# The low part of the in-projection weight by ScalarE and an adding transfer instead of VectorE

## The chip, the cores and the metric

The kernel runs on one core of a Trainium2 chip. The metric is the device time of one execution in microseconds (us). TensorE multiplies, VectorE and ScalarE do elementwise work, GpSimd and SyncE mainly issue transfers here. In the profile these are PE (PEld for its weight loads), DVE, ACT, POOL and SP; SPq and POOLq are the queues on which SP and POOL issue transfers.

## The reference

One layer of a diffusion backbone over 1024 latent tokens of width 1024, with 256 context tokens. All arithmetic is float32. Cut to what matters here:

```python
h = modulate(rmsnorm(x, norm1_g[i]), sh1, sc1)
q, k, v, hv, hx1, hx2, gna, ghy = jnp.split(h @ w_in[i], IN_SPLITS, axis=-1)
y_na = neighbourhood_attention(to_heads(q), to_heads(k), to_heads(v), ...)
y_hy = hyena_mixer(hv, hx1, hx2, *hy_params)
x = x + g1 * gated_merge(gna, ghy, y_na, y_hy, w_na_o[i], w_hy_o[i], w_out[i])
x = x + g2 * swiglu(modulate(rmsnorm(x, norm2_g[i]), sh2, sc2), ffn_w1[i], ffn_w3[i], ffn_w2[i])
return rmsnorm(x, final_g)
```

The change is inside `h @ w_in[i]`: a 1024 x 1024 activation times a 1024 x 5120 weight (the columns of k and v also multiply the 256 context tokens).

## The kernel before, in words

**A product in three parts.** A float32 product is made from operands that are split in two. The high part is the value rounded to the format that TensorE multiplies in (float32r); the low part is the value minus its high part. `gemm` (L187 to L198) then adds three products for each block of 128 rows: low weight by high activation, high weight by low activation, high by high, all three into one PSUM bank. `split` (L173 to L176) makes the parts: ScalarE casts the value into the high part (L175), VectorE subtracts the high part from the value (L176).

**A weight chunk.** The 5120 columns of `w_in` are 40 chunks of 128 columns. `weights` (L178 to L185) brings one in: SP issues a 512 KB load into the tile `wr` (L181), then `split` fills `wh` and `wl` (128 partitions x 1024 elements each). There is one buffer for `wr` and two each for `wh` and `wl`. So a chunk's parts can be written only when the chunk two before has been multiplied to its end, and its load can start only when the previous split has read `wr`.

**The order of chunks.** `project` (L574 and on) goes through the chunks in the order 4, 5, 6 to 23, 0 to 3, 32 to 39, 24 to 31. For each it asks for the weight of the next one, under a raised priority (L643 to L645), and then runs two halves of 512 tokens, 24 matmuls each, into the tile `in_ps`. ScalarE (L591 to L614), and for the short convolution also VectorE (L600), take a half out of its bank into the tile `proj`. For eight chunks a context product `ctx_ps` follows. Finished rows are stored by POOL (`qk` L624, `gate` L631, `hx`, `z`, `vtok` L572). The first two chunks, 4 and 5, are asked for in `hidden` (L305, L313), not in `project`.

**What runs beside it.** Between the chunks a merger of generators, with costs written out by hand, mixes in other work. First come the filters of the long convolution (`filt_ps` L363, which VectorE multiplies by a decay that SP loads into `dec`, L359; then `dft_ps` L442 to L444 from the tile `a`, which VectorE makes at L430) and the modulation rows (VectorE sums 64 loads `wal`, L887 to L890). Then come the convolutions. From about 640 us attention joins: POOL loads the tile `v` (L706, 64 loads of 64 KB in all), and a little later the matmuls of projection and attention are pinned to the order of the program and `in_ps` has one bank only. The rest of the order on each engine's queue is made by the framework when the kernel is built, by priorities and modelled durations; each queue then runs strictly in that order.

**After it.** The Hyena output projection, the merge, and the feed-forward stage use weights of their own; two of these also call `weights` with 512 columns.

Of the kernel before, what the change touches and what calls it, by code (L numbers as in the profile page):

```python
# [10 lines left out]
F32 = mybir.dt.float32  # L11
F32R = mybir.dt.float32r
AF = mybir.ActivationFunctionType
ALU = mybir.AluOpType
# [5 lines left out]
D = 1024  # L20
# [138 lines left out]
class Block:  # L159
# [15 lines left out]
        self.nc.scalar.copy(hi, src)  # L175
        self.nc.vector.tensor_sub(lo, src, hi.bitcast(F32))  # L176

    def weights(self, pool, src, n=D, tag="w"):  # L178
        nc = self.nc
        raw = pool.tile([P, D], F32, tag=tag + "r", name=tag + "r")[:, :n]  # L180
        nc.sync.dma_start(raw, src)  # L181
        hi = pool.tile([P, D], F32R, tag=tag + "h", name=tag + "h")[:, :n]
        lo = pool.tile([P, D], F32R, tag=tag + "l", name=tag + "l")[:, :n]
        self.split(hi, lo, raw)
        return hi, lo  # L185

    def gemm(self, ps, w, x, nk, width=512, pos=0, pin=False):  # L187
# [386 lines left out]
    def project(self, groups, wpool, psg, psc, hT, hcT, between, then):  # L574

        nc = self.nc
        count = [0]  # L580
        chunks = [f for g in groups for f in g]
        turn = []

        def half(f, w, st, ps, h):
            sl = slice(h * 512, (h + 1) * 512)
            count[0] += 1
            pt = psg[0 if self.pinned else count[0] % 2].tile([P, 512], F32, tag="g", name="in_ps")
            ps.append(pt)
            self.gemm(pt, w, hT[h], 8, 512, 0, self.pinned)
            if f < 4:  # L590
                nc.scalar.mul(st[:, sl].rearrange("p (c r i) -> p c r i", c=4, r=8),  # L591
                              pt.rearrange("p (r c i) -> p c r i", r=8, c=4), 0.125)
            elif f < 12:
                nc.scalar.copy(st[:, sl], pt)
            elif f < 24:
                c0, c1, c2, cb = (self.cw[:, f - 12, n:n + 1] for n in range(4))
                nc.scalar.activation(st[:, sl], pt, AF.Identity, bias=cb, scale=c1)

                def tap(d0, d1, src, c):
                    nc.vector.scalar_tensor_tensor(st[:, d0:d1], src, c, st[:, d0:d1], op0=ALU.mult, op1=ALU.add)  # L600

                with self.tc.high_priority():
                    if h == 0:
                        edge = self.stg.tile([P, 1], F32, tag="edge", name="edge")
                        nc.vector.tensor_copy(edge, ps[0][:, 511:512])
                        ps.append(edge)
                        tap(1, 512, ps[0][:, 0:511], c0)
                        tap(0, 511, ps[0][:, 1:512], c2)
                    else:
                        tap(512, 513, ps[1], c0)  # L610
                        tap(513, T, ps[2][:, 0:511], c0)
                        tap(511, T - 1, ps[2], c2)
            else:
                nc.scalar.activation(st[:, sl], pt, AF.Copy if f < 32 else AF.Sigmoid)  # L614

        def finish(f, w, st):
            if 4 <= f < 12:
                pc = psc.tile([P, 512], F32, tag="c", name="ctx_ps")
                self.gemm(pc[:, 0:TC], w, hcT, 8, TC)
            for t in turn:  # L620
                self.tokens(psc, *t)
            turn.clear()
            if f < 8:
                nc.gpsimd.dma_start(self.qkd[f], st)  # L624
            elif f < 12:
                turn.append((st, 8, self.vd.rearrange("(n p) c -> p n c", p=P)[:, :, (f - 8) * P:(f - 7) * P]))
            elif f < 24:
                g, cc = (f - 12) // 4, f % 4
                turn.append((st, 8, (self.zd[0] if g == 0 else self.hxd[g - 1])[cc // 2][:, :, (cc % 2) * P:(cc % 2 + 1) * P]))
            else:  # L630
                nc.gpsimd.dma_start(self.gd[f - 24], st)  # L631
            if 4 <= f < 12:
                sc = self.stc.tile([P, TC], F32, tag="oc", name="projc")
                nc.scalar.copy(sc, pc[:, 0:TC])
                if f < 8:
                    nc.gpsimd.dma_start(self.kcd[f - 4], sc)
                else:
                    turn.append((sc, 2, self.vcd.rearrange("(n p) c -> p n c", p=P)[:, :, (f - 8) * P:(f - 7) * P]))

        for group in groups:  # L640
            i = chunks.index(group[-1]) + 1
            for f in (*group, *chunks[i:i + 1]):
                if f not in self.ready:  # L643
                    with self.tc.high_priority():
                        self.ready[f] = self.weights(wpool, self.a["w_in"][f])  # L645
            ws = [self.ready.pop(f) for f in group]
            sts = [self.stg.tile([P, T], F32, tag="o", name="proj") for _ in group]
            pss = [[] for _ in group]
            for h in range(2):
                for f, w, st, ps in zip(group, ws, sts, pss):  # L650
                    half(f, w, st, ps, h)
                    if self.fine:
                        if h:
                            self.left -= 1
                            finish(f, w, st)
                        yield
                if group is groups[0]:
                    next(between)
                if group is groups[-1] and not h:
                    then()  # L660
            if not self.fine:
                for f, w, st in zip(group, ws, sts):
                    self.left -= 1
                    finish(f, w, st)
                    yield
# [806 lines left out]
```

## Time and profile before

| what | value |
|---|---|
| device time, median of 3 runs | 1711.23 us (1708.59 to 1711.89) |
| span of the profiled execution | 1711.4 us |
| splits of `w_in` chunks | 40, the first cast at 32.5 us |
| share of the span busy: PE, DVE, ACT, POOL | 97%, 72%, 39%, 9% |
| bytes moved by transfers | 282.48 MB, mean 165 GB/s |

The span is the profiled execution's own time; it lies 0.2 us beside the median of the runs. A row of the timeline has the start in us, the length in us, the engine, the line, what is written from what, and in brackets how long the engine had been idle and what ended that. A row of a table by stretches has, for each stretch, its length, the busy time of each engine, the granted clock of TensorE (PEclk, 1.00 is full), the busy share of the 16 DMA engines and GB/s. A row of the waits reads "who waited <- for what: us in total, how many times, the longest". A row of transfers ends with KB each and the median time from issue to landing.

### The profile page before, as it was taken

Reading aid. Unit: us, or ns where it says so; the run is one execution under the profiler, and the core shown is the slowest. Engines: PE = TensorE matmul, PEld = TensorE weight load, DVE = VectorE, ACT = ScalarE, POOL = GpSimd, SP = SyncE. Lnnn points to the kernel's source line nnn. Section 1 sums busy time; section 2 is a strip of 40 time slices with the busy share of each in tenths; the row PEclk is TensorE's granted clock in tenths of the full one; section 3 lists DMA queues with packets and bytes.
Section 4 is the critical chain, followed back from the end, with each engine's and each line's share of the span. In section 5 each row is a group of like instructions: output and inputs, shape, how many; then the busy total and the mean of one; then the engine's idle time right before and its main releaser. Section 6 shows DMA issues by size and latency. Waiting matters only on the chain.

```text
span 1711.4 us, 22611 instructions
## 1 busy us (share of the span) xinstructions
PE 1657.6 (97%) x8124; PEld 1307.2 (76%) x8124; DVE 1230.1 (72%) x2076; ACT 662.6 (39%) x1141; POOL 153.3 (9%) x274
## 2 busy tenths in 40 slices
PE   6898999999999999999999999999999999999997
PEld 2676776777777778888787888888888888878886
DVE  3697586699995966465865967867865566479576
ACT  4621221312221224455654315733333333355455
POOL 0100211101010014020200000010101011000000
PEclk9999999999999999999999999999999999999999
DMA  9276854645553456344657524333423223395334
GB/s 364 103 255 199 266 173 158 215 139 187 167 201 137 160 187 186 126 148 131 197 174 245 187 65 160 124 124 117 160 99 110 94 99 109 105 383 177 98 120 154
DMA packets 114517, 282.48 MB, mean 165 GB/s; under 512 B 15840, under 2 KB 24676, under 8 KB 112102
## 3 DMA queue, kind: packets, MB, share of 16 engines
q1 hardware_dynamic: 94472, 219.99, 38.6%
q0 software_dynamic: 19280, 60.60, 10.5%
q8 instruction: 64, 1.05, 0.3%
q10 hardware_dynamic: 653, 0.44, 0.1%
q14 instruction: 48, 0.39, 0.1%
HBM read 213.60 MB, written 67.39 MB: 164 GB/s over the span
## 4 chain that ended last, share of the span: by engine, by line
PE 65%; issue 10%; DVE 4%; DMA 2%; ACT 1%; POOL 1%; SPq 0%; DVEq 0%; POOLq 0%; ACTq 0%
PE x_ps L1171 15%; PE in_ps L195 12%; PE z_ps L1171 7%; PE dx_ps L1340 6%; PE out_ps L1109 4%; PE dz_ps L1340 3%; PE hy_ps L195 2%; PE y_ps L1171 2%; PE dft_ps L442 2%; PE pt_ps L800 2%; PE pt_ps L786 2%; PE na_ps L195 2%; PE dy_ps L1340 1%; PE s_ps L766 1%; PE dft_ps L444 1%
## 5 line engine op out<-in xcount | busy, mean ns | idle before, releaser
L195 PE MATMUL in_ps<-hTh,wl 128*128 128x512 f32 x640 | 260.0, 407 | 0.9 <-ACT proj L614 0.5
L195 PE MATMUL in_ps<-hTl,wh 128*128 128x512 f32 x640 | 254.5, 398 | 0.4 <-DVE hTl L176 0.2
L195 PE MATMUL in_ps<-hTh,wh 128*128 128x512 f32 x640 | 253.9, 397 | 0.0
L195 PEld LDWEIGHTS in_ps<-hTh,wl 128*128 128x128 f32 x640 | 121.5, 190 | 32.2 <-issue 5.6
L195 PEld LDWEIGHTS in_ps<-hTl,wh 128*128 128x128 f32 x640 | 121.8, 190 | 27.1 <-DVE hTl L176 1.8
L195 PEld LDWEIGHTS in_ps<-hTh,wh 128*128 128x128 f32 x640 | 121.6, 190 | 26.9 <-issue 0.4
L175 ACT CAST wh<-wr 128x1024 fp32r<-128x1024 f32 (+1 forms) x56 | 51.9, 926 | 141.4 <-PE in_ps L195 110.0
L176 DVE TENSOR_TENSOR wl<-wr,wh 128x1024 fp32r<-128x1024 f32 (+1 forms) x56 | 59.8, 1067 | 63.2 <-ACT wh L175 63.1
L176 DVE TENSOR_TENSOR ol<-ws,oh 128x512 fp32r<-128x512 f32 x88 | 60.4, 688 | 50.6 <-ACT oh L175 50.3
L176 DVE TENSOR_TENSOR ol<-ar,oh 128x512 fp32r<-128x512 f32 x77 | 52.8, 687 | 47.7 <-ACT oh L175 47.7
L175 ACT CAST oh<-ar 128x512 fp32r<-128x512 f32 x77 | 47.9, 622 | 84.4 <-PE dx_ps L1340 33.1
L175 ACT CAST oh<-ws 128x512 fp32r<-128x512 f32 x88 | 54.7, 622 | 57.1 <-PE x_ps L1171 27.5
L442 PE MATMUL dft_ps<-a,matf 128*128 128x512 f32 x128 | 67.1, 606 | 5.0 <-DVE a L430 4.1
L775 ACT ACTIVATE pe<-pe,mx 128x640 f32<-128x640 f32 x64 | 52.6, 822 | 48.9 <-DVE mx L774 48.9
L1340 PE MATMUL dx_ps<-ol,oh 128*128 128x512 f32 x176 | 68.7, 390 | 1.7 <-DVE ol L176 1.7
L774 DVE CUSTOM_DVE_ANT_0 pe<-s_ps,bias 128x640 f32<-128x640 f32 x64 | 50.1, 820 | 28.1 <-PE s_ps L769 28.1
L1340 PE MATMUL dx_ps<-oh,ol 128*128 128x512 f32 x176 | 67.4, 390 | 1.9 <-DVE ol L176 1.9
L1340 PE MATMUL dx_ps<-oh 128*128 128x512 f32 x176 | 68.5, 389 | 0.0
L176 DVE TENSOR_TENSOR ol<-wr,oh 128x512 fp32r<-128x512 f32 x70 | 48.0, 688 | 22.3 <-ACT oh L175 22.2
L175 ACT CAST oh<-wr 128x512 fp32r<-128x512 f32 x70 | 43.3, 622 | 52.3 <-PE x_ps L1171 16.0
L890 DVE SCALAR_TENSOR_TENSOR aacc<-wal,cs,aacc 128x512 f32<-128x512 f32 x56 | 41.8, 747 | 23.1 <-DMA wal<-in_w_ada 22.5
L1111 DVE TENSOR_TENSOR x<-x,out_ps 128x512 f32<-128x512 f32 x64 | 42.6, 683 | 15.2 <-PE out_ps L1109 15.0
(394 smaller groups left out, 4193.7 us busy)
## 6 DMA issues: line engine op xcount, KB each, us to landing
wr<-in_w SPq DMA_DIRECT2D x52, 512.0 KB, 3.4
wr<-in_w_in SPq DMA_DIRECT2D x40, 512.0 KB, 4.2
ar<-g SPq DMA_DIRECT2D x77, 256.0 KB, 2.8
wal<-in_w_ada SPq DMA_DIRECT2D x64, 256.0 KB, 4.1
matf<-in_dft_f SPq DMA_DIRECT2D x32, 384.0 KB, 4.7
bias<-in_rpb SPq DMA_DIRECT2D x64, 192.0 KB, 3.7
g<-t POOLq DMA_DIRECT2D x47, 256.0 KB, 3.0
w<-in_w SPq DMA_DIRECT2D x44, 256.0 KB, 5.4
```

The costliest lines, as they stand in the source:

```text
L175: self.nc.scalar.copy(hi, src)
L176: self.nc.vector.tensor_sub(lo, src, hi.bitcast(F32))
L195: mm = nc.tensor.matmul(ps, ww[:, k * P:(k + 1) * P], xx[:, k, pos:pos + width], start=(i == 0), stop=(i == n - 1))
L442: nc.tensor.matmul(ps, m[:, 0], v.rearrange("p a b -> p (a b)"), start=True, stop=False)
L774: nc.vector.tensor_tensor_reduce(pe, ps[:, 256:896], bt, -1.0, 3e38, ALU.add, ALU.min, mx[:, 0:1])
L775: nc.scalar.activation(pe, pe, AF.Exp, bias=mx[:, 0:1], scale=-1.0, accum_out=mx[:, 1:2])
L786: pin(nc.tensor.transpose(pt[:, at:at + P], pe[:, c * P:(c + 1) * P], self.ident))
L890: nc.vector.scalar_tensor_tensor(acc, w, c, acc, op0=ALU.mult, op1=ALU.add)
L1109: nc.tensor.matmul(ps, gg[x][:, tk], ww[y][:, sl], start=(i == 0), stop=(i == n - 1))
L1111: nc.vector.tensor_add(x1[:, sl], x1[:, sl], ps)
L1171: mm = nc.tensor.matmul(ps, w[u][:, k * P:(k + 1) * P], x[v][:, k, :], start=(start and k == 0 and i == 0), stop=(stop and k == 3 and i == 2),
L1340: nc.tensor.matmul(ps[j], x[u][:, j * P:(j + 1) * P], w[v], start=(start and i == 0 and c == 0), stop=(stop and i == N - 1 and k == len(re ...
```

## The change

`weights` gets a flag, and `project` sets it. With the flag, ScalarE casts the chunk into the high part as before, then writes minus the high part into the low part's tile, and POOL issues a transfer that reads the same 512 KB of the weight from memory a second time and adds it to what stands in that tile. VectorE's subtraction is gone for these chunks. Chunks 4 and 5 and all other weights keep `split`, so 38 of the 40 chunks change.

```diff
-    def weights(self, pool, src, n=D, tag="w"):
+    def weights(self, pool, src, n=D, tag="w", by_dma=False):
         nc = self.nc
         raw = pool.tile([P, D], F32, tag=tag + "r", name=tag + "r")[:, :n]
         nc.sync.dma_start(raw, src)
         hi = pool.tile([P, D], F32R, tag=tag + "h", name=tag + "h")[:, :n]
         lo = pool.tile([P, D], F32R, tag=tag + "l", name=tag + "l")[:, :n]
-        self.split(hi, lo, raw)
+        if by_dma:
+            nc.scalar.copy(hi, raw)
+            nc.scalar.mul(lo, hi.bitcast(F32), -1.0)
+            nc.gpsimd.dma_start(lo, src, accum_op=ALU.add)
+        else:
+            self.split(hi, lo, raw)
         return hi, lo
...
                 if f not in self.ready:
                     with self.tc.high_priority():
-                        self.ready[f] = self.weights(wpool, self.a["w_in"][f])
+                        self.ready[f] = self.weights(wpool, self.a["w_in"][f], by_dma=True)
```

## The prediction

> **What bounds the kernel now.** I read the page's head first, then the busy time by stretches, then what TensorE (PE) waits for.
>
> ```profile
> span 1711.4 us, 22611 instructions
> ...
> PE 1657.6 (97%) x8124; PEld 1307.2 (76%) x8124; DVE 1230.1 (72%) x2076; ACT 662.6 (39%) x1141; POOL 153.3 (9%) x274
> ```
>
> PE is busy for 97% of the span, VectorE (DVE) for 72%. An average over stages says nothing about this change, so here is the stage in which the changed chunks are multiplied (columns: stretch and its length, busy PE, PEld, DVE, ACT, POOL, granted clock, share of the DMA engines, GB/s).
>
> ```profile
> 30.00:100.00 70.00, 62.73 (x328) 47.40 (x325) 48.46 (x80) 39.00 (x66) 6.79 (x14) 0.98 0.50 177
> 100.00:200.00 100.00, 92.74 (x432) 68.58 (x431) 78.31 (x113) 20.18 (x35) 13.21 (x24) 0.97 0.72 237
> 200.00:300.00 100.00, 93.81 (x441) 70.72 (x440) 71.82 (x97) 23.07 (x37) 11.92 (x17) 0.95 0.56 177
> 300.00:400.00 100.00, 99.85 (x421) 74.39 (x421) 84.50 (x151) 26.35 (x39) 8.74 (x13) 1.00 0.55 180
> 400.00:500.00 100.00, 100.00 (x425) 75.73 (x424) 95.63 (x162) 24.98 (x35) 10.12 (x15) 1.00 0.55 184
> ```
>
> From 300 us on PE has no idle time to give back, although VectorE is at its fullest there (95.63 of 100 us). Only up to 300 us does PE idle: 7.27 + 7.26 + 6.19 = 20.7 us. The waits of PE from 100 to 300 us, and then all of them from 300 to 815 us:
>
> ```profile
> PE filt_ps L363 <- DVE fv L370: 7.8, 2, 4.3
> PE dft_ps L442 <- DVE a L430: 2.8, 2, 1.9
> ```
>
> ```profile
> PE dft_ps L442 <- DVE a L430: 1.3, 1, 1.3
> PE in_ps L195 <- ACT proj L614: 0.5, 1, 0.5
> PE dft_ps L442 <- issue: 0.2, 1, 0.2
> ```
>
> So after 300 us PE waits 2.0 us in all, and never for a low part `wl`. What a cheaper `wl` can win lies before 300 us. What it can lose lies wherever `wl` comes late.
>
> **What the change removes.** VectorE loses one subtraction for each of 38 chunks. The row below counts 40, of which the first is the early chunk 5 and the last belongs to a later weight:
>
> ```profile
> L176 DVE TENSOR_TENSOR wl<-wr,wh x40: 670/1224/1226, 45.0 to 808.5; 128x1024 fp32r<-128x1024 f32 x39, 128x512 fp32r<-128x512 f32 x1
> ```
>
> 38 x 1.22 = 46 us of VectorE. Most of it is beside a full PE and is worth nothing. One case stands ahead of something PE waits for:
>
> ```profile
> 230.68 1.22 DVE L176 TENSOR_TENSOR wl<-wr,wh 128x1024 fp32r<-128x1024 f32 x1
> ```
>
> The instructions behind it end in `a`, for which PE waits 2.8 us in two waits (above). I take 2.0 us of these as a gain; the bounds are 0 and, if queues that run ahead shorten other stalls too, 5.
>
> **What it adds on ScalarE.** One pass of 128 x 1024 elements for each chunk. The nearest row is such a scaled copy:
>
> ```profile
> L458 ACT ACTIVATE wp<-u x4: 1058/1062/1062, 330.7 to 560.5; 128x1024 f32<-128x1024 f32 x4
> ```
>
> 38 x 1.06 = 40 us, on an engine that is busy for 20 to 39 us of the stretches above. Queued behind it on ScalarE are the copies that empty `in_ps`. Here that matters once, where the product has gone over to one bank:
>
> ```profile
> 666.26 1.05 ACT L175 CAST wh<-wr 128x1024 fp32r<-128x1024 f32 x1 [1.03 <-PE in_ps L195]
> 667.22 0.59 ACT L614 ACTIVATE proj<-in_ps 128x512 f32<-128x512 f32 x1
> ...
> 667.86 5.79 PE in_ps L195 x24
> ```
>
> PE starts when the bank is empty. With the new pass between the two ScalarE instructions, it starts 1.05 us later; 0 if the copy is queued first. I take 1.05.
>
> **What it adds as a transfer.** No row shows an adding transfer. Near it are POOL's stores of 256 and 512 KB and its one 512 KB load, at the start among other large loads (median us from issue to landing, last):
>
> ```profile
> g<-t POOLq DMA_DIRECT2D x47, 256.0 KB, 3.0
> ...
> gate<-proj POOLq DMA_DIRECT2D x16, 512.0 KB, 3.8
> ...
> fw<-in_fw POOLq DMA_DIRECT2D x1, 512.0 KB, 9.7
> ```
>
> 256 KB more cost 0.8 us, so moving 512 KB costs 1.6. An add must also read what stands in the tile: 3.8 + 1.6 = 5.4. I take 6 us, an estimate from these rows, because this stage's DMA share is above average; bounds 3.8 and 9.7. The Trainium skill, "DMA: Bandwidth & Descriptors", section "Anatomy of one DMA", fits such a transfer with 2.0 us plus the bytes at 436 GB/s: 3.2 us for the plain copy (the trace has 3.8), and by my second reading of the same bytes an estimate of 4.4. By that figure the one late chunk below would be in time and the sum 0.9 us less.
>
> **Does `wl` come late?** Until now it was there one cast and one subtraction after the buffers came free, 1.05 + 0.1 + 1.22 = 2.4 us. Now it is cast, pass, 0.1, transfer: 1.05 + 1.05 + 0.1 + 6 = 8.2 us, so 5.8 us later. For each changed chunk I took the time from the end of its subtraction to its first matmul. In 35 of 38 it is 9.7 us or more; the least of these:
>
> ```profile
> 398.07 1.21 DVE L176 TENSOR_TENSOR wl<-wr,wh 128x1024 fp32r<-128x1024 f32 x1
> ...
> 409.02 0.48 PE L195 MATMUL in_ps<-hTh,wl 128*128 128x512 f32 x1
> ```
>
> 409.02 - 399.28 = 9.7. The product of the chunk before covers 5.8 us there; without that cover each chunk would cost 5.8 us. Two of the three others follow each other in the short stretch where little other work stands between chunks:
>
> ```profile
> 646.65 1.05 ACT L175 CAST wh<-wr 128x1024 fp32r<-128x1024 f32 x1
> ...
> 647.99 1.22 DVE L176 TENSOR_TENSOR wl<-wr,wh 128x1024 fp32r<-128x1024 f32 x1
> ...
> 655.07 0.40 PE L195 MATMUL in_ps<-hTh,wl 128*128 128x512 f32 x1
> ...
> 655.27 1.05 ACT L175 CAST wh<-wr 128x1024 fp32r<-128x1024 f32 x1 [0.28 <-PE in_ps L195]
> ...
> 657.65 6.50 POOL L706 DMA_DIRECT2D v<-vtok  x12
> ...
> 660.34 1.21 DVE L176 TENSOR_TENSOR wl<-wr,wh 128x1024 fp32r<-128x1024 f32 x1
> ```
>
> The first of them: 646.65 + 2.2 = 648.85. POOL is issuing loads of `v`, 6.50 / 12 = 0.54 us each; two in front make 1.1. Landing 648.85 + 1.1 + 6 = 655.95, needed at 655.07: 0.9 us late (0 to 4.6). The second: 655.27 + 2.2 + 6 = 663.5, needed at 667.86: in time, because the subtraction itself had waited for VectorE. If POOL's queue puts it behind the twelve loads, 664.15 + 6 = 670.15, 2.3 us late. The raised priority speaks for in front: I take 0.
>
> The third is chunk 6, early in the stage:
>
> ```profile
> 76.82 1.04 ACT L175 CAST wh<-wr 128x1024 fp32r<-128x1024 f32 x1 [2.01 <-PE ctx_ps L195]
> ...
> 82.99 0.39 PE L195 MATMUL in_ps<-hTh,wl 128*128 128x512 f32 x1
> ...
> 85.51 1.29 DVE L370 TENSOR_TENSOR fv<-filt_ps,dec 128x512 f32<-128x512 f32 x2 [3.49 <-DMA dec<-in_decay]
> 86.26 1.13 PE L363 MATMUL filt_ps<-fw,hid 64*128 64x256 f32 x6 [2.42 <-DVE fv L370]
> ```
>
> 76.82 + 2.2 + 6 = 85.0, needed at 82.99, 2.0 us late. But three matmuls later PE waits anyway until 86.26 for `filt_ps`, which hides it. That second wait has a transfer behind it, `dec`, and this is the last term.
>
> **The traffic.** 38 x 0.524 MB = 20 MB more are read from memory. PE's stalls before 300 us follow transfers, as at 86.26 (above) and here:
>
> ```profile
> 141.46 1.39 DVE L370 TENSOR_TENSOR fv<-filt_ps,dec 128x512 f32<-128x512 f32 x2 [3.67 <-DMA dec<-in_decay]
> ...
> 142.21 2.07 PE L363 MATMUL filt_ps<-fw,hid 64*128 64x256 f32 x6 [4.33 <-DVE fv L370]
> ...
> 265.27 2.07 PE L363 MATMUL filt_ps<-fw,hid 64*128 64x256 f32 x6 [3.48 <-DVE fv L370]
> ```
>
> ```profile
> 125.00:129.00 4.00, 3.80 (x13) 2.20 (x12) 3.59 (x6) 2.01 (x4) 0.55 (x1) 1.00 1.00 357
> ...
> 137.00:141.00 4.00, 0.87 (x4) 0.38 (x2) 0.75 (x1) 0.00 (x0) 0.00 (x0) 1.00 0.91 299
> 141.00:145.00 4.00, 2.79 (x8) 1.87 (x9) 3.20 (x5) 0.00 (x0) 0.00 (x0) 0.62 0.69 237
> ...
> 259.00:264.00 5.00, 2.80 (x19) 1.83 (x18) 0.26 (x1) 1.35 (x3) 1.72 (x3) 1.00 0.93 313
> ```
>
> While PE stands still the DMA engines are at 0.91 to 1.00 and 299 to 357 GB/s. So they, not VectorE, hold these three stalls, and 0.524 MB more at 299 GB/s lengthens each by 1.75 us: 5.25 us. The bounds are 0, if the addition is through before `dec` is asked for, and 10.5, if the second reading counts in full. A long stall also costs clock: 0.62 in the 4 us after it. The Trainium skill, "DMA: Bandwidth & Descriptors", section "Issuing engines are not separate DMA queues", speaks against the change in the same way, since POOL's transfers interleave on the 16 engines that serve SP's; the rows above agree.
>
> **Sum.** -2.0 (VectorE) + 1.05 (bank) + 0.9 (one late chunk) + 5.25 (traffic) = +5.2 us, on the profiled 1711.4: 1716.6 us. The median of the runs, 1711.23, lies 0.2 below the span, which I neglect.
>
> **The rivals.**
>
> *All of it is hidden.* The transfers pass in gaps and the late chunk is caught by the merger's other work: 1711, within 2 us. For it: 35 of 38 chunks have 9.7 us of cover. Against: the full DMA engines at the three stalls.
>
> *VectorE was the limit before 300 us, so the kernel gets faster.* Ten of the changed chunks are split there, 12 us of VectorE at 70 to 78% busy. If each subtraction stands in the chain that feeds `filt_ps` or `dft_ps`, up to 8 of the 20.7 us of idle PE go: 1703. For it: PE names VectorE in nearly all these waits. Against: VectorE itself names a transfer, 3.49 and 3.67 us. It decides if the DMA engines are below full at the stalls.
>
> *The adding transfer is long.* At 9.7 us chunk 6 starts at 88.7 and `filt_ps` 0.7 later, +3.1; the tight chunks +4.6 and, behind the `v` loads, 664.15 + 9.7 - 667.86 = +6.0; traffic twice, +10.5; with the bank's 1.05 and the gain of 2.0 it is +23: 1734. All others are still covered (5.8 + 3.7 = 9.5, below 9.7); beyond that length every chunk of the convolution stage begins to pay.
>
> A rule of the Trainium skill, "SBUF — State Buffer", section "Who interferes with whom", would add to this: a transfer that GpSimd issues cannot get its descriptors written while VectorE runs an instruction that takes both of its ports. If it bites, it delays an issue by one such instruction, by the rows above at most about 1.2 us; no run here shows it.
>
> Each case has some 3 us of play, since the queues' order is made anew from modelled durations, and no trace of before shows that.
>
> **How the numbers follow.** Chances: the forecast 0.46 (its own range 1712 to 1722), hidden 0.25, VectorE 0.14, long transfer 0.15. A measurement of this kernel tells about 0.2%, 3.4 us, from no change. Slower by more: 0.40 of the forecast's 0.46 and all of the long transfer, 0.55. Within: 0.21 of hidden and 0.06 of the forecast, 0.27. Faster: 0.14, and 0.04 of hidden by a luckier order, 0.18. The range 1706 to 1729 leaves out about 0.08 below and 0.10 above.
>
> **What would show it.** Right: landing of the added transfer at 5 to 7 us; VectorE's busy time down by about 46 us and ScalarE's up by 40; PE's idle time before 300 us up by some 4 us, with DMA shares near 1 at the stalls; after 300 us one or two new waits of PE, for a transfer into `wl` or for `proj`, around 655 to 668 us. Wrong: landings near 10 us with PE waiting for `wl` at many chunks; or PE's idle time before 300 us shrinking with VectorE's load; or no new wait anywhere.

## The result, and the profile after

| | median of the runs | ratio to before (95% interval) |
|---|---|---|
| before | 1710.82 us (1708.59 to 1711.89, 4 runs) | |
| after | 1733.68 us (1732.91 to 1737.49, 4 runs) | 1.0145 [1.0126, 1.0164] |

The change costs 22.9 us. The forecast was 5.2 us, with 1729 as the upper end of its range: the direction is right, the size is not. The ratio on record is not the quotient of the two medians, which is 1.0134; by the ratio the loss is 24.8 us, and the experiments below are compared by their ratios. The profiled execution after took 1732.91 us, 1.9 more than its span. The page after, head, transfers and the new issue (its last number is the median landing):

```profile
span 1731.0 us, 22679 instructions
...
PE 1660.7 (96%) x8124; PEld 1308.5 (76%) x8124; DVE 1188.8 (69%) x2038; ACT 695.2 (40%) x1179; POOL 189.0 (11%) x312
...
q0 software_dynamic: 24752, 80.53, 16.4%
...
wl<-in_w_in POOLq DMA_DIRECT2D x38, 512.0 KB, 7.3
```

The edit did what it says: 38 instructions moved from VectorE to ScalarE, VectorE's busy time fell by 41 us and ScalarE's rose by 33, and POOL's queue carries 19.9 MB more. The span of the page grew by 19.6 us. Span minus busy PE is PE's idle time: 53.8 us before, 70.3 after, so 16.5 us of the 19.6 are idle time, and 3.1 are longer busy time of PE with the same number of matmuls. Where the idle time lies is in the tables by stretches (length, busy PE, PEld, DVE, ACT, POOL, granted clock, DMA share, GB/s):

```profile
30.00:100.00 70.00, 61.45 (x312) 46.17 (x309) 44.88 (x76) 40.28 (x67) 8.58 (x16) 0.95 0.55 187
100.00:200.00 100.00, 89.27 (x417) 64.67 (x415) 73.92 (x108) 23.71 (x38) 14.96 (x24) 0.97 0.79 248
200.00:300.00 100.00, 90.85 (x422) 68.65 (x421) 59.19 (x86) 24.45 (x38) 16.26 (x24) 0.95 0.67 203
300.00:400.00 100.00, 98.25 (x414) 72.30 (x413) 76.26 (x138) 30.31 (x43) 14.30 (x19) 1.00 0.61 185
...
600.00:700.00 100.00, 93.56 (x432) 74.17 (x430) 58.90 (x113) 34.13 (x52) 28.93 (x48) 1.00 0.68 191
```

Between 30 and 300 us PE idles for 8.55 + 10.73 + 9.15 = 28.4 us; it was 20.7. The DMA share in those stretches rose from 0.72 to 0.79 and from 0.56 to 0.67, and VectorE, with less to do, waits more: its busy time from 200 to 300 us is 59 us, not 72. Two of the stalls in close-up:

```profile
190.00:194.00 4.00, 0.21 (x1) 0.24 (x2) 0.72 (x2) 0.96 (x2) 1.99 (x3) 0.91 1.03 397
270.00:274.00 4.00, 0.70 (x2) 0.29 (x2) 0.36 (x1) 0.86 (x2) 0.76 (x1) 1.00 0.94 335
```

PE, VectorE and ScalarE are nearly idle; only the DMA engines are full. The first of these stalls ends for PE with a load of the matrix `matf`, for which it waited 0.6 us in one wait before:

```profile
193.78 2.05 PE L447 MATMUL dft_ps<-a,matf 128*128 128x512 f32 x2 [3.81 <-DMA matf<-in_dft_f]
```

The second place is the attention stage. In windows of 10 us from 640 us on:

```profile
640.00:650.00 10.00, 10.00 (x54) 8.33 (x53) 9.67 (x18) 3.55 (x5) 1.97 (x3) 1.00 0.90 306
650.00:660.00 10.00, 8.24 (x37) 6.48 (x36) 4.12 (x8) 3.55 (x7) 5.20 (x10) 1.00 1.03 312
660.00:670.00 10.00, 10.00 (x45) 8.05 (x44) 6.42 (x11) 4.41 (x7) 7.38 (x13) 1.00 0.95 211
670.00:680.00 10.00, 7.64 (x34) 5.94 (x33) 7.78 (x15) 4.12 (x6) 2.76 (x6) 1.00 0.65 222
680.00:690.00 10.00, 7.68 (x42) 6.08 (x41) 3.77 (x10) 5.51 (x8) 6.66 (x13) 1.00 1.03 256
```

Here 6.4 us of PE are lost between 650 and 690 us, where before it lost 0.55. What PE waits for over the whole trace, among others:

```profile
PE filt_ps L368 <- DVE fv L375: 6.7, 3, 2.6
PE dft_ps L447 <- DVE a L435: 6.6, 6, 3.7
...
PE in_ps L200 <- DMA wl<-in_w_in: 4.6, 2, 2.3
PE in_ps L200 <- ACT proj L619: 4.1, 2, 2.4
```

PE waits for the low part itself in two places only, 4.6 us in all. The rest of the added idle time has other names, so a late `wl` alone does not explain the result.

### The profile page after: what moved, and what is told of

Same layout as the page of the kernel before. It is cut to its first block, busy times and chain, and to the rows that moved or that the text cites. A ratio compares the mean times of both kernels' runs of the same rounds, so it can differ in the third digit from the quotient of the medians.

```text
span 1731.0 us, 22679 instructions
## 1 busy us (share of the span) xinstructions
PE 1660.7 (96%) x8124; PEld 1308.5 (76%) x8124; DVE 1188.8 (69%) x2038; ACT 695.2 (40%) x1179; POOL 189.0 (11%) x312
## 3 DMA queue, kind: packets, MB, share of 16 engines
q0 software_dynamic: 24752, 80.53, 16.4%
## 4 chain that ended last, share of the span: by engine, by line
PE 54%; issue 22%; DMA 11%; DVE 8%; POOL 2%; ACT 2%; SPq 0%; POOLq 0%; DVEq 0%; ACTq 0%
PE in_ps L200 16%; PE out_ps L1114 5%; PE dx_ps L1345 5%; PE dft_ps L447 4%; PE x_ps L1176 3%; PE dz_ps L1345 3%; PE hy_ps L200 2%; PE dft_ps L448 2%; PE dft_ps L449 2%; PE na_ps L200 2%; DMA wal<-in_w_ada 2%; PE pt_ps L805 2%; PE pt_ps L791 2%; DMA wl<-in_w_in 1%; POOL g L1289 1%
## 5 line engine op out<-in xcount | busy, mean ns | idle before, releaser
L185 ACT CAST wh<-wr 128x1024 fp32r<-128x1024 f32 x38 | 39.8, 1047 | 134.7 <-PE in_ps L200 112.2
L780 ACT ACTIVATE pe<-pe,mx 128x640 f32<-128x640 f32 x64 | 52.5, 821 | 40.7 <-DVE mx L779 40.7
L187 POOL DMA_DIRECT2D wl<-in_w_in x38 | 34.3, 902 | 257.0 <-ACT wl L186 256.7
```

The costliest lines, as they stand in the source:

```text
L185: nc.scalar.copy(hi, raw)
L780: nc.scalar.activation(pe, pe, AF.Exp, bias=mx[:, 0:1], scale=-1.0, accum_out=mx[:, 1:2])
```

## The experiments

The theory: the transfers keep the 16 DMA engines busy, an add longer than its bytes suggest, and whatever else needs them before 300 us, and again around 650 us, comes later. The rivals: the low part is late; the order of the queues, which is made anew for each version; ScalarE's extra pass; and VectorE's relief, which would pull the other way. All ratios are against the kernel before on the same chip.

### The copy in place of the add

```diff
-            nc.gpsimd.dma_start(lo, src, accum_op=ALU.add)
+            nc.gpsimd.dma_start(lo, src)
```

> The changed kernel, but the second transfer only copies the weight over the low part's tile instead of adding to it (the addition is left out: the low part is the weight itself). The order of all queues is the changed kernel's, to the instruction; only the reading of the tile by the transfer is gone. Theory A (the add itself is slow, landing after 7.3 us instead of about 4, and the DMA engines pay for it twice): landing 4 to 5 us, and most of the 22.9 us go, time 1715 to 1721. Theory B (the bytes read a second time from memory, or the extra pass on ScalarE, or the new order of the queues): landing may fall, but the time stays at 1728 to 1734.

Measured: 1720.71 us, ratio 1.0072 [1.0057, 1.0086]. The page's transfer lines:

```profile
q0 software_dynamic: 24752, 80.53, 14.0%
...
wl<-in_w_in POOLq DMA_DIRECT2D x38, 512.0 KB, 6.0
```

This kernel and the changed one have the same instructions in the same order on every queue, and the same packets and bytes from POOL. They differ in the add alone, and it is worth half of the loss, 1.45% against 0.72%. The share of q0 times the span gives the time for which it occupies all 16 engines: before 10.5% of 1711.4 = 180 us, here 14.0% of 1716.1 = 240 us, after 16.4% of 1731.0 = 284 us. Over 38 transfers that is 1.6 us for a copy of 512 KB and 2.7 us for an add of it. The expectation of theory A is met in part: the time is inside its range, at the upper end, but only half of the loss is gone, and the landing is 6.0 us, not 4 to 5.

### ScalarE's pass without the transfer

```diff
-            nc.gpsimd.dma_start(lo, src, accum_op=ALU.add)
+            nc.vector.tensor_add(lo, lo.bitcast(F32), raw)
```

> The same result without the transfer: ScalarE writes minus the high part into the low part's tile, VectorE adds the weight to it. VectorE's load is that of before, ScalarE's that of the changed kernel, no byte is added. Theory A or traffic: the time is before's or within 3 us of it, 1709 to 1714, PE never waits for a transfer into the low part. Theory C (the extra pass on ScalarE, 1.06 us a chunk and the copies queued behind it): a good part of the loss is there, 1718 to 1726.

Measured: 1714.05 us, ratio 1.0024 [1.0009, 1.0039]. The pass and a new order of the queues, which is not quite that of the changed kernel, cost about 4 us with no added transfer at all. Its timeline around its one large late wait:

```profile
662.51 0.62 ACT L175 CAST krh<-kraw 128x512 fp32r<-128x512 f32 x1 [6.49 <-DVE kraw L702]
663.04 0.59 ACT L619 ACTIVATE proj<-in_ps 128x512 f32<-128x512 f32 x1
...
666.68 0.79 PE L200 MATMUL in_ps<-hTh,wl 128*128 128x512 f32 x1 [6.73 <-ACT proj L619]
```

On ScalarE's queue the cast of an attention key `krh` stands ahead of the copy that empties `in_ps`. The cast waits 6.49 us for a key, and PE, whose pinned order needs the one bank, stands still. This is the bank term of the prediction by another cause: not the new pass of 1.05 us, but what the order puts ahead of the copy.

### Traffic alone

The split stays with VectorE, and POOL stores the finished low part to a scratch in memory that nobody reads.

```diff
-            nc.scalar.copy(hi, raw)
-            nc.scalar.mul(lo, hi.bitcast(F32), -1.0)
-            nc.gpsimd.dma_start(lo, src, accum_op=ALU.add)
+            self.split(hi, lo, raw)
+            nc.gpsimd.dma_start(self.idle[len(self.idle_n) % 2], lo.bitcast(F32))
+            self.idle_n.append(1)
```

> The kernel before (ScalarE casts, VectorE subtracts), and behind each subtraction of the 38 chunks POOL stores the low part to a scratch in memory that nobody reads: 38 x 512 KB more through the DMA engines and POOL's queue, with nobody waiting for it except the next write of the tile. Theory T (traffic at the DMA-full stretches before 300 us): PE's idle time before 300 us grows as in the changed kernel, 1716 to 1722. Theory A with lateness as the cause: within 3 us of before, 1709 to 1714.

Measured: 1721.45 us, ratio 1.0074 [1.0057, 1.0090].

```profile
q0 software_dynamic: 24752, 80.53, 13.4%
...
idle<-wl POOLq DMA_DIRECT2D x38, 512.0 KB, 6.1
```

Transfers that no product waits for cost 12.7 us. The order of the queues is not what costs here: in the traces PE and VectorE run their instructions in exactly the order of the kernel before, and ScalarE, POOL and SP differ from it only in a few places (on POOL, for one, a `gate` store goes ahead of two loads of `v`).

### Relief without the transfer

The transfer and the addition are left out; VectorE is relieved, ScalarE has its pass.

```diff
             nc.scalar.mul(lo, hi.bitcast(F32), -1.0)
-            nc.gpsimd.dma_start(lo, src, accum_op=ALU.add)
```

> The changed kernel without the transfer (the addition of the weight is left out: the low part is minus the high part). VectorE is relieved by 46 us, ScalarE has its pass, no byte is added, nothing is late. If VectorE was the limit before 300 us: 1703 to 1707. If VectorE's time is worth nothing, as PE's full stretches say: 1709 to 1713. If the extra pass on ScalarE or a new order of the queues costs: 1716 or more.

Measured: 1708.94 us, ratio 1.0007 [0.9996, 1.0019]. With 38 subtractions gone, 41 us of VectorE's busy time, and ScalarE's pass in their place, nothing is won that these runs can tell. The stretches:

```profile
30.00:100.00 70.00, 64.42 (x338) 48.48 (x331) 48.09 (x78) 40.89 (x68) 7.19 (x15) 0.97 0.51 179
100.00:200.00 100.00, 94.21 (x440) 69.49 (x440) 75.28 (x113) 23.55 (x38) 12.87 (x24) 0.98 0.76 249
200.00:300.00 100.00, 95.87 (x457) 71.88 (x456) 72.89 (x106) 29.84 (x47) 12.99 (x19) 0.98 0.56 178
```

This run also answers the rival of the new order. In the traces PE, VectorE and SP run in exactly the order of the changed kernel; ScalarE and POOL, the adds aside, differ in a few places. So what the change loses against this run, 1.0145 to 1.0007, is the work of the transfers: the relief, the pass and the new order together come to 0.07%. PE idles for 15.5 us between 30 and 300 us here and for 28.4 us in the changed kernel.

That 15.5 is less than the 20.7 before, but the relief is not shown to be the reason: in the run in which VectorE adds the weight, and so keeps its load, it is 16.4. Here 3.5 us are lost between 640 and 700 us, where before 0.55 were.

### The change for a part of the chunks

```diff
-                        self.ready[f] = self.weights(wpool, self.a["w_in"][f], by_dma=True)
+                        self.ready[f] = self.weights(wpool, self.a["w_in"][f], by_dma=6 <= f < 16)
```

The other two have the conditions `16 <= f < 24 or f < 4 or 32 <= f < 38` and `24 <= f < 32 or f >= 38`; the three together are the 38 chunks.

> The change for chunks 6 to 15 alone, the ten whose transfers run beside the filters and the modulation rows, before 300 us; all others keep VectorE's subtraction. If the loss is made where the DMA engines are full: +8 to +11 us against before, about half of the whole. If it is made by late low parts wherever little work stands between chunks: +0 to +3.

> The change for chunks 16 to 23, 0 to 3 and 32 to 37 alone, eighteen in the convolution stage, from 300 to about 640 us, where PE has no idle time and the cover is 9.7 us or more. Both theories: +0 to +3 us, the transfers land within their cover. A loss of 8 or more would mean that the cost is per chunk and not by place.

> The change for chunks 38, 39 and 24 to 31 alone, the ten beside the start of attention, where POOL also issues the loads of v. If late low parts and POOL's queue count there: +4 to +6 us, with PE waiting for the low part's transfer or for the bank of in_ps between 640 and 690 us. If all of the loss is traffic before 300 us: +0 to +2.

| chunks | median | ratio | loss per chunk, mean |
|---|---|---|---|
| 10 early (to about 290 us) | 1727.16 us | 1.0099 [1.0084, 1.0114] | 1.7 us |
| 18 middle | 1712.22 us | 1.0009 [0.9991, 1.0026] | 0.1 us |
| 10 late (from about 640 us) | 1715.69 us | 1.0034 [1.0021, 1.0047] | 0.6 us |

The percentages add up to 1.42, the whole change's 1.45 within the intervals. Two thirds of the loss come from ten chunks. The same step on the 18 in the middle, where PE is full and the share of the DMA engines was about 0.5, costs nothing measurable.

By the medians the early ten cost 17.5 us, well over the 8 to 11 that were expected; the middle and the late ones, 2.5 and 6.0 us, are within what was expected. The 1.7 us are the whole run's loss spread over ten chunks, not a delay seen at each: in the trace of the early run PE idles for 29.4 us between 30 and 300 us, 8.7 more than before; it idles for 3.4 us between 640 and 700 us, where no chunk is changed and before it was 0.55; and it is busy for 1662.1 us, 4.5 more.

### The source in SBUF instead of memory

```diff
-            nc.gpsimd.dma_start(lo, src, accum_op=ALU.add)
+            nc.gpsimd.dma_start(lo, raw, accum_op=ALU.add)
```

> The changed kernel, but the adding transfer takes the weight from the tile that SP has loaded instead of from memory: 20 MB less are read from memory, as many bytes go through the DMA engines. The tile is held until the addition has landed, so the next chunk's load starts some 6 us later. If bytes from memory are the cost: 1715 to 1722. If the time that an addition takes on the 16 DMA engines is the cost (2.7 us of all of them, by the queue's share): still 1726 to 1734 or more.

Measured: 1746.38 us, ratio 1.0216 [1.0202, 1.0231]. Nothing is read from memory twice, and yet the share of q0 is as high and the time higher:

```profile
q0 software_dynamic: 24752, 80.53, 16.8%
...
wl<-wr POOLq DMA_DIRECT2D x38, 512.0 KB, 5.6
```

So the second reading of memory is not the cost. The engines' time is no less, 3.0 us for each add by the same working, and in addition the one buffer of `wr` is held until the add has landed, so the next chunk's load starts later. That this hold is the whole of the further 12 us was not tried by itself.

### The add alone, with nobody waiting for it

As in the run with stores, but adding to the scratch (the first two are stored).

```diff
-            nc.gpsimd.dma_start(self.idle[len(self.idle_n) % 2], lo.bitcast(F32))
+            nc.gpsimd.dma_start(self.idle[len(self.idle_n) % 2], lo.bitcast(F32),
+                                **(dict(accum_op=ALU.add) if len(self.idle_n) > 1 else {}))
```

> The split by VectorE is kept, so no product waits for the transfer and ScalarE gets no pass. Instead each changed low part is added by a GpSimd transfer to a scratch in memory that nobody reads (the first two are stored, 36 are added). It is the run with the plain stores (ratio 1.0074) with an add in place of each store. Theory A, an add is dear because it occupies the DMA engines longer than a plain transfer (2.74 us of all 16 engines against 1.3 to 1.6), whoever waits for it: q0's share goes from 13.4% to about 16.5%, and the time to the whole change's, ratio 1.012 to 1.016 (1730 to 1737 us). Rival B, the change is dear because products wait for a late low part and because the queues are ordered anew; the engines' time matters little: as the plain stores, ratio 1.006 to 1.009 (1720 to 1725), whatever the share of q0.

Measured: 1734.59 us, ratio 1.0148 [1.0125, 1.0170]. Its head, and then its stretches:

```profile
span 1726.5 us, 22673 instructions
...
q0 software_dynamic: 24752, 80.53, 16.9%
...
idle<-wl POOLq DMA_DIRECT2D x38, 512.0 KB, 8.1
```

```profile
30.00:100.00 70.00, 62.29 (x321) 46.37 (x316) 46.84 (x78) 38.42 (x65) 8.07 (x16) 0.97 0.52 186
100.00:200.00 100.00, 89.77 (x421) 65.96 (x420) 79.07 (x114) 20.09 (x34) 15.54 (x26) 0.97 0.83 252
200.00:300.00 100.00, 87.95 (x412) 66.20 (x412) 62.80 (x87) 20.84 (x34) 15.43 (x22) 0.93 0.67 200
```

This is the run that decides. VectorE does all its subtractions, ScalarE has no pass, no product waits for a transfer, and every queue has the order of the run with stores, so PE and VectorE have the order of the kernel before. In the trace no instruction of PE, VectorE or ScalarE waits for one of these transfers or for POOL; on POOL itself a load of `v` and a store of `gate` wait for them, 6.9 us in all. Still the whole loss of the change is there, and PE idles for 30.0 us between 30 and 300 us. The rivals that the loss comes from the late low part, or from the new order, fall. Twice now, in two pairs of kernels with equal queues, an add in place of a plain transfer has added 0.73 to 0.74%.

### GpSimd subtracts

A complete kernel that was meant to relieve VectorE with no added transfer.

```diff
-            nc.scalar.mul(lo, hi.bitcast(F32), -1.0)
-            nc.gpsimd.dma_start(lo, src, accum_op=ALU.add)
+            nc.gpsimd.tensor_sub(lo, raw, hi.bitcast(F32))
```

> The changed chunks' low parts are subtracted by GpSimd instead of VectorE: VectorE is relieved of all 38 subtractions, the computation is whole, and there is no transfer and no ScalarE pass. Theory A, the relief of VectorE is worth nothing, since transfers hold the stalls before 300 us: ratio 0.998 to 1.002 (1706 to 1713 us), if GpSimd's subtraction takes up to some 6 us. Rival B, VectorE's 46 us are worth something that the run without any addition hid by chance: 1700 to 1705. If GpSimd's subtraction holds up the transfers that GpSimd issues behind it, or is much longer than 6 us, it is slower than A: 1715 or more.

Measured: 1748.77 us, ratio 1.0250 [1.0227, 1.0273], the slowest of all, although the subtraction takes only 2.7 us on GpSimd. It is no test of VectorE's relief, because VectorE was not relieved: its busy time is 1233.0 us, against 1230.1 before, with 38 instructions fewer. The same group on VectorE, in the trace before and in this one:

```profile
L600 DVE SCALAR_TENSOR_TENSOR proj<-edge,cw,proj 128x1 f32<-128x1 f32 x12 | 2.5, 211 | 0.0
```

```profile
L604 DVE SCALAR_TENSOR_TENSOR proj<-edge,cw,proj 128x1 f32<-128x1 f32 x12 | 19.9, 1655 | 19.5 <-ACT proj L601 19.5
```

And one of the twelve beside GpSimd's instruction:

```profile
261.62 2.34 POOL L186 TENSOR_TENSOR wl<-wr,wh 128x1024 fp32r<-128x1024 f32 x1 [14.16 <-ACT wh L185]
262.25 1.74 DVE L604 SCALAR_TENSOR_TENSOR proj<-edge,cw,proj 128x1 f32<-128x1 f32 x1 [2.49 <-ACT proj L601]
```

An instruction on 128 x 1 elements starts at 262.25 and ends at 263.99, just after GpSimd's ends at 263.96. How much of the 2.5% comes from such holds was not worked out.

### The kernel before, profiled again

> The kernel before, profiled once more, to see how far places and times of PE's stalls move from one profiled execution to the next with the program unchanged. Every theory: span 1704 to 1715 us, PE's idle time before 300 us 14 to 21 us. If it moves by more than that, differences of single stalls between profiles carry no verdict.

Measured: one time of 1706.53 us.

```profile
span 1704.1 us, 22611 instructions
...
PE 1651.6 (97%) x8124; PEld 1303.4 (76%) x8124; DVE 1230.5 (72%) x2076; ACT 662.2 (39%) x1141; POOL 153.3 (9%) x274
```

The span is 7.3 us shorter than that of the first profile, nearly all of it in busy PE (1651.6 and 1657.6 us); the idle time is 52.5 and 53.8 us. PE's idle time between 30 and 300 us is 19.8 us, against 20.7. So the idle times compare within some 1 us between these two profiles, and the spans only to some 7 us. Against this second profile the change has 17.8 us more idle time, and its matmuls take 9.1 us longer.

## Why the prediction was wrong

**What bounds the kernel.** Right: after 300 us PE was full, and the middle chunks cost nothing there. But the prediction took the whole time after 300 us as one, and looked at the attention stage only through the two tight chunks.

**VectorE, -2.0 us.** Not seen, and not measured by itself. Relief, pass and new order together gave 1.0007 [0.9996, 1.0019], where this term and the next one add up to a gain of 0.95 us. In the changed kernel VectorE's busy time fell by 41 us, but between 30 and 300 us it waits longer for its own transfers. Its waits from 70 to 300 us, after, for the 256 KB loads `wal` (before: 22.5 us in all):

```profile
DVE aacc L895 <- DMA wal<-in_w_ada: 32.6, 19, 6.0
...
DVE aacc L897 <- DMA wal<-in_w_ada: 4.6, 3, 2.4
```

**The bank of `in_ps`, +1.05 us.** Right place, wrong cause and size. PE waits for this copy 4.1 us in two waits. The timeline of the longer one, after:

```profile
670.94 0.01 DVE L694 LOAD_MASK_SELECT shuf<-kraw  x1 [3.93 <-DMA kraw<-qk]
...
673.51 0.69 DVE L702 TENSOR_TENSOR kraw<-kraw,shuf 128x512 f32<-128x512 f32 x1
...
674.24 0.62 ACT L175 CAST krh<-kraw 128x512 fp32r<-128x512 f32 x1 [6.58 <-DVE kraw L702]
...
675.71 0.59 ACT L619 ACTIVATE proj<-in_ps 128x512 f32<-128x512 f32 x1
...
676.35 0.50 PE L200 MATMUL in_ps<-hTh,wl 128*128 128x512 f32 x1 [2.36 <-ACT proj L619]
```

Read it upwards: PE waits for the copy, the copy stands behind the cast of a key, the cast waits for VectorE, VectorE for a load. A late load and a queue's order make the stall together. No added transfer is needed for it: in the relief run, with the same order on PE and VectorE, PE waits for this copy 4.2 us in three waits and loses 3.5 us between 640 and 700 us. So of the 6.4 us after, some 3 more than there are the transfers' (2.3 of them the wait for `wl` shown below), as far as single executions tell. The adds in the order of before cost PE 3.5 us between 650 and 700 us.

**The landing, 6 us, and the late chunks, +0.9 us.** Near. The median landing is 7.3 us: above the 6 taken, below the 9.7 of the rival, and in the quietest stretch the 5.4 worked out from the stores was right. Here are the landings from 300 to 480 us, after, and with the copy:

```profile
wl<-in_w_in POOLq DMA_DIRECT2D x9, 512.0 KB, 5.5
```

```profile
wl<-in_w_in POOLq DMA_DIRECT2D x9, 512.0 KB, 4.2
```

From 100 to 300 us the medians are 7.1 and 5.2. The fit that the prediction cited from the Trainium skill, "DMA: Bandwidth & Descriptors", section "Anatomy of one DMA", would have 3.2 us for the copy and by the prediction's estimate 4.4 for the add; the trace has 4.2 and 5.5 at its quietest, so both lie about 1 us above it here. The 32nd chunk, charged 0.9 us, cost nothing: its add landed as PE finished the chunk before. The 33rd, charged 0, made PE wait; the timeline after:

```profile
677.54 0.91 POOL L187 DMA_DIRECT2D wl<-in_w_in  x1 [0.39 <-ACT wl L186]
...
685.52 0.47 PE L200 MATMUL in_ps<-hTh,wl 128*128 128x512 f32 x1 [2.32 <-DMA wl<-in_w_in]
```

So one late chunk there is right, at 2.3 us in place of 0.9, but it is the other one.

**Chunk 6, +0.** Wrong. The prediction hid its lateness behind a wait for `filt_ps` that came "three matmuls later". After the change that wait stands before it in PE's queue:

```profile
79.36 0.95 POOL L187 DMA_DIRECT2D wl<-in_w_in  x1
...
84.53 1.13 PE L368 MATMUL filt_ps<-fw,hid 64*128 64x256 f32 x6 [2.03 <-DVE fv L375]
...
88.22 0.80 PE L200 MATMUL in_ps<-hTh,wl 128*128 128x512 f32 x1 [2.25 <-DMA wl<-in_w_in]
```

The add was issued at 79.36 and its product began at 88.22, 8.9 us later, in a stretch full of loads. PE pays both waits. A cover that consists of a place in a queue is gone when the queue is ordered anew.

**The traffic, +5.25 us, bounds 0 to 10.5.** This is the step that failed, and it carries the miss: the transfers were charged for 5.25 us of traffic and 0.9 us of lateness, and cost 1.38% beyond the relief run, about 23.6 us. The prediction saw rightly that "they, not VectorE, hold these three stalls", and that the transfers pay there. Two things in "0.524 MB more at 299 GB/s lengthens each by 1.75 us" were wrong. First the price: 299 GB/s is the rate of loads, and an add of 512 KB occupies all engines for 2.7 us. That alone would have made 3 x 2.7 = 8.1 us, still inside the bounds. Second, and more, the count: it charged three existing stalls once each, and nothing elsewhere. The ten early chunks cost 1.7 us each in the mean, and the ten late ones 0.6 us each, at a place where PE had lost 0.55 us before. Adds that no product waits for gave 25.3 us by their ratio; the upper bound had been 10.5. The traces show later loads, in VectorE's longer waits for `wal` and PE's for `matf`; they do not show which add delayed which load, so that part is inferred.

One more term was named and not charged: "A long stall also costs clock". PE's busy time grew by 3.1 us against the first profile of before and by 9.1 against the second, and the granted clock of the span was 0.988, against 0.993 in both. As the two profiles of before differ by 6.0 us themselves, the size of this term stays open.

**The rivals.** "All of it is hidden" falls by the ratio of the change. "VectorE was the limit" falls as well: without the transfers the relief came to no gain, and with them PE idles more before 300 us while VectorE does less. "The adding transfer is long" named 1734 us, and 1733.68 was measured; that the two agree is luck, because its sum is not what happened: it needed landings of 9.7 us and had tight chunks pay 4.6 and 6.0 us, while PE waits for `wl` 4.6 us in all, and the run in which no product waits is as slow. Its "traffic twice" was the one part in the right direction. The rule of the Trainium skill, "SBUF — State Buffer", section "Who interferes with whom", that VectorE's two-port instructions hold up GpSimd's transfers, is neither shown nor excluded by these runs: the same loss appears with VectorE's 38 subtractions kept (1.0148) and removed (1.0145), so these do not make it, but VectorE's other instructions were the same in both.

## What to carry to other kernels

Price a transfer that is added to a busy stage by the engine time that it occupies, and set that against the stage's DMA share, not against whether its own result is late: in the mean the same add cost 1.7 us a chunk where the DMA engines held up PE and 0.1 where PE was full. Taking 41 us off VectorE, which before 300 us waits for transfers, won nothing that could be measured here, and sending that work to the DMA engines put it onto the bottleneck. A hiding place that rests on the order of a queue has to be charged as open when the order is made anew.

## What the hardware showed beyond this

- An add of 512 KB by a transfer occupies the 16 DMA engines for 2.7 us, a copy for 1.6 (1.3 for a store from SBUF), with the same packets and bytes counted on q0. In the other runs with adds the same working gives 2.5 to 3.0 us; with the source in SBUF instead of memory it is 3.0 (16.8% on q0). Its landing is about 1.3 us longer in the quiet stretch.
- A GpSimd instruction of 2.3 us held a VectorE instruction that otherwise takes 0.21 us until its own end; in the mean of twelve 1.66 us. The Trainium skill, "SBUF — State Buffer", section "Who interferes with whom", has the cause as a port pair that the two share and that one of them locks for a whole instruction; this trace agrees, in this direction.
